# A state space layer: the input product and 6 of the 16 outputs of the gated product in plain float32, these 6 summed chunk by chunk beside the states

## The chip, the cores and the metric

The program runs on one NeuronCore of a Trainium2 chip. The metric is the time of one execution on the device in microseconds (us). The engines that matter here are TensorE (PE, the matrix multiplier, with its weight loads PEld), VectorE (DVE), ScalarE (ACT), GpSimd (POOL), and SyncE (SP), which issues most of the transfers. Each runs its own list of instructions in order, and waits on semaphores for the others. DVE and ACT do elementwise work; PE's sums land in PSUM, eight banks of 2 KB for each of the 128 partitions.

## The reference, cut to what matters

Two models run one after the other. The change is in the second, which has four layers on a sequence of 256 positions and 1024 channels. Each layer is a mixer and a gated feed-forward (`swiglu`), each behind a root-mean-square norm. The mixers are attention (layer 0), the state space layer (1), a pooling layer (2), attention (3).

```python
def s5_layer(h, w_in, a_re, a_im, log_dt, b_re, b_im, c_re, c_im, d, w_glu):
    u = (h @ w_in).astype(F32)
    u_g = u.reshape(B, S, S5_GROUPS, S5_GROUP).astype(jnp.complex64)
...
    bu = jnp.einsum('gpc,bsgc->bsgp', b_bar, u_g)
...
    _, states = lax.associative_scan(combine, (lam_seq, bu), axis=1)
...
    y = jnp.einsum('gcp,bsgp->bsgc', c_mat, states).real.reshape(B, S, D_MODEL)
    y = y + d.astype(F32) * u
    g = jax.nn.gelu(y).astype(h.dtype)
    val, gate = jnp.split(g @ w_glu, 2, axis=-1)
    return val * jax.nn.sigmoid(gate)
```

`w_in` is 1024 x 1024 and `w_glu` 1024 x 2048. There are 64 groups of 16 channels with 64 complex states each. All inputs are float32.

## The kernel before

Activations lie with channels on the partitions: `x[:, k]` is one of eight chunks (KC = 8) of 128 channels by 256 positions (T). A product of a weight tile and an activation is made as three matmuls (`mm3`, L48) in the reduced format fp32r. Each operand is split into a high part and the rest: `piece` (L66) makes `wh` on ACT (a copy in fp32r) and `wl` on DVE (raw minus `wh`) from a raw weight tile that `raw` (L61) loads with a transfer of 1024 KB. The products are wh by high, wh by low and wl by high, and a block of 128 outputs needs 8 x 3 of them. One wh and one wl cover 128 outputs by all 1024 inputs (128x1024). The plain `mm` (L46) on float32 operands is also in the program, in the norms (`ones` as weights).

Around the state space layer, `block2` (L1541 to L1546) calls `s5_table` (it builds tables on POOL and ACT), then `ffn(0)`, the feed-forward of layer 0, then `s5`, then the pooling layer with `ffn(1)`. The Tile scheduler writes each engine's list in the order in which the code issues instructions, with priorities for a few. `s5_table` stands in the code ahead of `ffn(0)`, and so its ACT instruction for `rtab` (tile s5rt, L2125), which copies the decay factor of all 32 state blocks over 128 positions (128x4096), stands on ACT ahead of the first reciprocal root of the norm in `ffn(0)`, `rstd`.

`s5` (L2172) goes through the eight chunks m of 128 channels (eight groups, 512 states). For each chunk:
- **The input product**: `wh`, `wl` of one 128-column piece of `w_in`, and 24 matmuls into a PSUM bank. The activation was left by `prep` (L1594) of `ffn(0)` as two tiles `gh` (ACT) and `gl` (DVE). DVE multiplies by the norm's `rstd` into `u` (L2240).
- **States**: PE makes `bu` from `u` and the transfer `bc` (32 matmul instructions, 32 rows each). DVE multiplies it by a table (tiles `A`, L2197, and `B`, L2198), POOL adds the halves into `Z` (L2199), DVE scans `Z` twice with `rtab` (L2204) and turns it back by the table (again tiles `A` and `B`, L2206 and L2207; each tile name has two buffers). PE makes the outputs of the chunk from `A`, `B`, `u` (72 small matmuls), DVE adds the direct term (`yy`, L2218), ACT takes the gelu, and `split` leaves `yh`, `yl`.
- The three stages of neighbouring chunks overlap by generators (`turn`), which are stepped once a chunk.

After the last input product, `linear` (L1688) makes the 16 blocks of 128 outputs of the gated product (the values m and the gates m of pair m, eight pairs), each from a `wh` and a `wl` piece. A written plan starts the first three of them with the chunks that are ready while the last states run. `emit` (L2249) applies the gate, adds to `x`, and prepares the next norm.

## Time and profile before

| What | us |
|---|---|
| Median of 3 runs | 2117.79 |
| Lowest and highest of the 3 | 2117.03, 2118.68 |
| Time of the profiled execution | 2118.83 |
| Its span in the trace | 2117.0 |
| PE busy, share of the span | 1964.3, 93% |
| DVE busy, share | 1436.8, 68% |
| ACT busy, share | 1044.2, 49% |
| POOL busy, share | 405.9, 19% |

The span is the time from the first to the last instruction in the trace; the time of the execution is 1.83 us longer. Busy shares are means over a program with many different stages, so whether an engine bounds a stage must be read from the windows of that stage. In the span's clock (us from its start), `ffn(0)` begins at about 1050 and `s5` runs from about 1246 to 1384. A matmul's start, and the distance from one start to the next, tell more than its recorded duration, as matmuls are pipelined and overlap.

### The profile page before, as it was taken

The page shows a single profiled execution, that of the slowest core. Times are in us where ns is not written, and L with a number is a line of the kernel's source. Part 1 is how long each engine was busy: PE and PEld are TensorE (multiplying, and loading weights), DVE is VectorE, ACT ScalarE, POOL GpSimd, SP SyncE. Part 2 cuts the span into 40 slices and gives each one's busy share as a digit, 9 for nine tenths or more (in the row PEclk, how much of TensorE's full clock was granted, in tenths as well). Part 3 has the DMA queues.
Part 4 walks back from the last instruction along what each step waited for, and adds up shares of the span by engine and source line. Part 5 has one row for each costly group of instructions (what it writes and reads, how often), then busy time and mean ns, then how long its engine had stood idle before and what let it go on. Part 6 is the DMA issues. An engine that isn't in the chain of part 4 may idle for free.

```text
span 2117.0 us, 36711 instructions
## 1 busy us (share of the span) xinstructions
PE 1964.3 (93%) x14800; PEld 1697.8 (80%) x14803; DVE 1436.8 (68%) x2407; ACT 1044.2 (49%) x1766; POOL 405.9 (19%) x562
## 2 busy tenths in 40 slices
PE   6999897999899879899899996899999999999998
PEld 3666465998585655488899985899999999989998
DVE  4999548998783541298766679866558656767654
ACT  4445635886544531276544442354456444555444
POOL 1001212234100110133289812200010000010000
PEclk9999997999999989999999998999999999999999
DMA  7665136999327959945556552365535554436551
...
DMA packets 275714, 408.87 MB, mean 193 GB/s; under 512 B 10000, under 2 KB 241424, under 8 KB 268240
## 3 DMA queue, kind: packets, MB, share of 16 engines
...
q8 instruction: 119, 1.95, 0.4%
...
HBM read 390.93 MB, written 24.64 MB: 196 GB/s over the span
## 4 chain that ended last, share of the span: by engine, by line
PE 49%; DVE 7%; issue 3%; ACT 2%; POOL 1%; DMA 1%; SPq 0%; DVEq 0%; POOLq 0%; ACTq 0%
PE mm L46 44%; PE gu L46 3%; DVE wl L55 2%; DVE Z L2204 1%; PE py L46 1%; PE px L46 1%; DVE gl L1600 1%; DMA rawx<-in_w_up 1%; POOL x L1580 1%; ACT wh L54 0%; DVE A L2197 0%; PE mm L1833 0%; DMA raw<-in_fox_w_in 0%; DVE A L2206 0%; POOL Z L2199 0%
## 5 line engine op out<-in xcount | busy, mean ns | idle before, releaser
L55 DVE TENSOR_TENSOR wl<-raw,wh 128x1024 fp32r<-128x1024 f32 x476 | 584.3, 1232 | 214.4 <-ACT wh L54 212.2
L54 ACT ACTIVATE wh<-raw 128x1024 fp32r<-128x1024 f32 x476 | 496.4, 1050 | 468.7 <-PE mm L46 263.1
L46 PE MATMUL mm<-gh,wh 128*128 128x256 f32 (+1 forms) x1744 | 497.6, 285 | 2.6 <-ACT wh L54 2.6
L46 PE MATMUL mm<-gh,wl 128*128 128x256 f32 (+1 forms) x1744 | 494.9, 284 | 3.3 <-DVE wl L55 3.3
L46 PE MATMUL mm<-gl,wh 128*128 128x256 f32 (+1 forms) x1744 | 493.9, 283 | 0.3 <-DVE gl L1600 0.3
L46 PEld LDWEIGHTS mm<-gh,wh 128*128 128x128 f32 (+1 forms) x1744 | 330.2, 189 | 6.1 <-ACT wh L54 3.0
L46 PEld LDWEIGHTS mm<-gh,wl 128*128 128x128 f32 (+1 forms) x1744 | 329.8, 189 | 4.9 <-DVE wl L55 4.3
L46 PEld LDWEIGHTS mm<-gl,wh 128*128 128x128 f32 (+1 forms) x1744 | 329.9, 189 | 1.3 <-DVE gl L1600 0.5
L46 PE MATMUL mm<-fh,wh 128*128 128x256 f32 x704 | 199.2, 286 | 3.0 <-DVE x L1640 1.6
L46 PE MATMUL mm<-fl,wh 128*128 128x256 f32 x704 | 199.0, 284 | 0.0
L46 PE MATMUL mm<-fh,wl 128*128 128x256 f32 x704 | 198.5, 284 | 0.0
L1604 POOL TENSOR_TENSOR sq<-sq 128x256 f32<-128x256 f32 x48 | 40.0, 834 | 682.1 <-ACT sq L1602 484.3
L46 PEld LDWEIGHTS mm<-fh,wh 128*128 128x128 f32 x704 | 134.3, 192 | 5.1 <-DVE x L1640 2.4
L46 PEld LDWEIGHTS mm<-fl,wh 128*128 128x128 f32 x704 | 135.0, 192 | 0.3 <-DVE fl L55 0.2
L46 PEld LDWEIGHTS mm<-fh,wl 128*128 128x128 f32 x704 | 134.7, 192 | 0.0
L46 PE MATMUL gu<-wh,gt 128*128 128x256 f32 (+1 forms) x576 | 109.5, 298 | 0.2 <-DVE gt L55 0.2
L1666 DVE TENSOR_TENSOR ft<-mm,rstd 128x512 f32<-128x512 f32 x88 | 60.8, 691 | 52.1 <-PE mm L46 52.1
L54 ACT ACTIVATE fh<-fa 128x256 fp32r<-128x256 f32 x88 | 36.7, 417 | 111.0 <-DVE fa L1669 111.0
L46 PEld LDWEIGHTS gu<-wh,gt 128*128 128x128 f32 (+1 forms) x576 | 87.0, 185 | 3.4 <-DVE gt L55 0.4
L46 PE MATMUL gu<-wl,gt 128*128 128x256 f32 (+1 forms) x320 | 85.6, 311 | 1.3 <-DVE wl L55 1.2
L46 PE MATMUL proj<-xh,wh 128*128 128x512 f32 x208 | 85.1, 410 | 0.0
L46 PE MATMUL proj<-xh,wl 128*128 128x512 f32 x208 | 83.0, 399 | 0.0
...
## 6 DMA issues: line engine op xcount, KB each, us to landing
raw<-in_ffn_w_gate_up SPq DMA_DIRECT2D x88, 1024.0 KB, 5.5
raw<-in_w_ada SPq DMA_DIRECT2D x48, 1024.0 KB, 6.0
raw<-in_ffn_w_down SPq DMA_DIRECT2D x44, 1024.0 KB, 4.9
raw<-in_w_down SPq DMA_DIRECT2D x26, 1024.0 KB, 11.3
raw<-in_fox_w_in SPq DMA_DIRECT2D x24, 1024.0 KB, 5.7
raw<-in_w_in SPq DMA_DIRECT2D x20, 1024.0 KB, 5.4
raw<-in_w_up SPq DMA_DIRECT2D x16, 1024.0 KB, 11.2
raw<-in_w_gate SPq DMA_DIRECT2D x15, 1024.0 KB, 12.3
```

The costliest lines, as they stand in the source:

```text
L46: return self.nc.tensor.matmul(out, a, b, start=start, stop=stop, skip_group_check=True)
L54: self.nc.scalar.activation(hi, src, AF.Copy)
L55: (lo_eng or self.nc.vector).tensor_tensor(lo, src, hi.bitcast(F32), op=ALU.subtract)
L1580: nc.gpsimd.tensor_tensor(x, x, self.rs1, op=ALU.mult)
L1600: nc.vector.scalar_tensor_tensor(self.gl[:, k], x, s, self.gh[:, k].bitcast(F32), op0=ALU.mult, op1=ALU.subtract)
L1604: nc.gpsimd.tensor_tensor(sq, sq, self.sq, op=ALU.add)
L1666: nc.vector.tensor_tensor(t, gu, rs[:, None, :].to_broadcast([P, 2, T]), op=ALU.mult)
L2204: nc.vector.tensor_tensor_scan(z, self.rtab[:, 4 * m:4 * m + 4].rearrange("p a t -> p (a t)"), z, 0.0, ALU.mult, ALU.add)
```

## The change

Five things change; the numbers of lines are those of the changed kernel only in the rows below.

1. **The input product** is 8 plain float32 matmuls a chunk on the weights as loaded, in place of 24 in fp32r. No `wh`, `wl` are made of `w_in`. Its activation is one float32 tile `gf`, which ACT writes in `ffn(0)`; the eight DVE instructions for `gl` go.
2. **Six of the 16 blocks** of the gated product (the pairs 0 to 2, NA = 3) are summed chunk by chunk, as plain float32 matmuls of `yy` on rows of `w_glu` as loaded (`rows`, two transfers of 384 KB for two chunks), into three PSUM banks `acc`. The other ten keep `piece` and `mm3`.
3. **PSUM**: one bank `mm` is shared by the input products and the outputs (there were four), three are `acc`, and `bu` keeps four, which the later blocks take over.
4. **The order** within a chunk is written out in `step(m)`.
5. **`rtab`** is two tiles of four state blocks, written by eight ACT instructions (128x4x127), one for a chunk, in place of one of 128x4096.

```diff
-                with banks(4) as self.pm, tc.tile_pool(name="s5t", bufs=1) as st:
+                    self.ffn(0, self.V["mix"][1], whole=True)
+                with banks(1) as self.pm, tc.tile_pool(name="s5t", bufs=1) as st:
...
         if g is not None:
-            self.gh, self.gl = self.b8("gh"), self.b8("gl")
+            self.gh, self.gl = (self.b8("gf", F32), None) if whole else (self.b8("gh"), self.b8("gl"))
...
             nc.scalar.activation(self.gh[:, k], x, AF.Copy, scale=s)
-            nc.vector.scalar_tensor_tensor(self.gl[:, k], x, s, self.gh[:, k].bitcast(F32), op0=ALU.mult, op1=ALU.subtract)
+            if self.gl is not None:
+                nc.vector.scalar_tensor_tensor(self.gl[:, k], x, s, self.gh[:, k].bitcast(F32), op0=ALU.mult, op1=ALU.subtract)
...
 
-        self.rtab = sp.tile([P, NS, P], F32, name="s5rt")
-        nc.scalar.activation(self.rtab, self.s5r[:, :, None].to_broadcast([P, NS, P]), AF.Copy)
-        nc.gpsimd.memset(self.rtab[:, :, 0:1], 0.0)
+        self.rtab = [sp.tile([P, 4, P], F32, name=f"s5rt{q}") for q in range(2)]
...
+
+        NA = 3
+        accs = lambda: self.pm.tile([P, 2, T], F32, name="acc", tag="acc", bufs=NA)
+        sums, rows, raw = [], {}, {}
...
             bu = bu[:, :, 0:2].rearrange("p a q t -> p q a t")
-            tab = self.tab[:, 4 * m:4 * m + 4].rearrange("p a q t -> p q a t")
             A, B, Z = t("A", four), t("B", four), t("Z", four, 1)
-            nc.vector.tensor_tensor(A, bu, tab, op=ALU.mult)
-            nc.vector.tensor_tensor(B, bu, tab[:, ::-1], op=ALU.mult)
+            nc.vector.tensor_tensor(A, bu, tab(m), op=ALU.mult)
+            done = nc.vector.tensor_tensor(B, bu, tab(m)[:, ::-1], op=ALU.mult)
             nc.gpsimd.tensor_tensor(Z[:, 0], A[:, 0], A[:, 1], op=ALU.add)
             nc.gpsimd.tensor_tensor(Z[:, 1], B[:, 1], B[:, 0], op=ALU.subtract)
-            yield
+            nc.scalar.activation(self.rtab[m % 2][:, :, 1:], self.s5r[:, 4 * m:4 * m + 4, None].to_broadcast([P, 4, P - 1]), AF.Copy)
...
+        def scanned(m, Z):
             for q in range(2):
                 z = Z[:, q].rearrange("p a t -> p (a t)")
-                nc.vector.tensor_tensor_scan(z, self.rtab[:, 4 * m:4 * m + 4].rearrange("p a t -> p (a t)"), z, 0.0, ALU.mult, ALU.add)
+                done = nc.vector.tensor_tensor_scan(z, self.rtab[m % 2].rearrange("p a t -> p (a t)"), z, 0.0, ALU.mult, ALU.add)
...
+        def rest(m):
+            nc.vector.tensor_tensor(yl[:, m], ys[m], yh[:, m].bitcast(F32), op=ALU.subtract)
+
+        def summed(k):
+
+            if not sums:
+                sums.extend(accs() for _ in range(NA))
+            for m in range(NA):
+                for q in range(2):
+                    self.mm(sums[m][:, q], rows[k // 2][:, k % 2, q, m * P:m * P + P], ys[k], k == 0 and q == 0, k == KC - 1)
+
+        after = lambda d: self.tc.issue_after(d.ins)
+        ab = {}
+
+        def step(m):
+
+            k = m - 1
+            done = None
+            if 0 <= k < KC:
+                Z, done = states(k)
+            if k > 1:
+                y = outputs(k - 2, *ab.pop(k - 2))
+                if done:
+                    with after(done):
+                        activated(k - 2, y)
+                else:
+                    activated(k - 2, y)
+            if m < KC:
+                ps = product(m)
+            if 0 <= k < KC:
+                done = scanned(k, Z)
+            if m < KC:
+                done = nc.vector.tensor_tensor(us[m], halves(ps), halves(self.rs), op=ALU.mult)
+            if done:
+                with after(done):
+                    if k > 1:
+                        rest(k - 2)
+                    if 0 <= k < KC:
+                        ab[k] = turned(k, Z)
+            elif k > 1:
+                rest(k - 2)
+            if k > 1:
+                summed(k - 2)
+
...
+        def product(m):
             if m % 2 == 0:
-                raw = self.raw(w[:, :, P * m:P * m + 256], KC, 256)
-            wh, wl = self.piece(raw[:, :, m % 2 * P:m % 2 * P + P], [KC, P])
+                raw[0] = self.raw(w[:, :, P * m:P * m + 256], KC, 256)
+                r = rows[m // 2] = self.wp.tile([P, 2, 2, NA * P], F32, name="raw", tag="raw", bufs=self.wbufs[0])
+                for kk in range(2):
...
             for k in range(KC):
-                self.mm3(ps, wh[:, k], wl[:, k], self.gh[:, k], self.gl[:, k], k == 0, k == KC - 1)
+                self.mm(ps, raw[0][:, k, m % 2 * P:m % 2 * P + P], self.gh[:, k], k == 0, k == KC - 1)
...
-            nc.vector.tensor_tensor(g, ps[0], g, op=ALU.mult)
-            nc.vector.tensor_tensor(self.x[:, m], self.x[:, m], g, op=ALU.add)
-            self.prep(m)
+                    self.norm(lambda: accs()[:, 0])
+            return ps
+
+        for m in range(KC):
+            step(m)
...
+        raws, open_, banks = {}, {}, []
+
+        def part(c, k0, k1):
+            m, q = divmod(c, 2)
+            if c not in open_:
+                if m % 2 == 0:
+                    at = q * D + (NA + m) * P
+                    n = min(256, D - (NA + m) * P)
+                    raws[q] = self.raw(wg[:, :, at:at + n], KC, n)
+                if c == 0:
+                    b = self.pm.tile([P, 4, 2, T], F32, name="bu", tag="bu", bufs=1)
+                    banks.extend(b[:, a] for a in range(4))
+                if c == 8:
+                    banks.append(accs())
+                open_[c] = self.piece(raws[q][:, :, m % 2 * P:m % 2 * P + P], [KC, P])
+            wh, wl = open_[c]
+            for k in range(k0, k1):
+                self.mm3(banks[m][:, q], wh[:, k], wl[:, k], yh[:, k], yl[:, k], k == 0 and q == 0, k == KC - 1)
+
         self.prep_begin(gnext)
-        self.linear([wg[:, :, q * D:q * D + D] for q in range(2)], yh, yl, emit, rest(), (None, (0, 0, 5), None, (1, 0, 5), (2, 0, 5), (0, 5, 6), (1, 5, 6), None, (2, 5, 6), (0, 6, 7), (1, 6, 7), (2, 6, 7)))
+        step(KC)
+        for c in range(3):
+            part(c, 0, 5)
+        step(KC + 1)
+        for c in range(3):
+            part(c, 5, 7)
+        step(KC + 2)
+        for m in range(NA):
+            emit(m, sums[m])
+        for c in range(2 * (KC - NA)):
+            part(c, 7 if c < 3 else 0, KC)
+            if c % 2:
+                emit(NA + c // 2, banks[c // 2])
         self.prep_end()
```

ACT at the start of `ffn(0)`, with the semaphores that each row waits for (DMASW are transfers that POOL issued, here the stores of `s5_table`'s inputs). Before:

```order
L54 ACTIVATE wh_10537<-raw_10454 128x1024 [waits PE_49,Activation_49]
L1599 ACTIVATE gh_9846<-x_58,cols_6818 128x256 [waits DVE_49]
L1602 ACTIVATE sq_10151<-x_58 128x256 [waits Pool_49]
L2125 ACTIVATE s5rt_10168<-s5r_8430 128x4096 [waits DMASW5_49,DMASW4_49,DMASW6_49,DMASW3_49,DMASW2_49]
L1584 ACT_TABLE_LOAD
L1584 ACTIVATE rstd_10480<-mm_10477,eps_94 128x256 [waits PE_49]
L54 ACTIVATE wh_10565<-raw_10456 128x1024 [waits PE_49,Activation_49]
L54 ACTIVATE wh_10637<-raw_10630 128x1024 [waits DMAHW5_49,PE_49,Activation_49]
```

and now:

```order
L54 ACTIVATE wh_10538<-raw_10455 128x1024 [waits PE_49,Activation_49]
L1600 ACTIVATE gh_9846<-x_58,cols_6818 128x256 [waits DVE_49]
L1604 ACTIVATE sq_10151<-x_58 128x256 [waits Pool_49]
L54 ACTIVATE wh_10533<-raw_10459 128x1024 [waits DMASW5_49,DMASW6_49,DMASW4_49,DMAHW4_49,DMASW3_49,DMASW2_49]
L1584 ACT_TABLE_LOAD
L1584 ACTIVATE rstd_10481<-mm_10478,eps_94 128x256 [waits PE_49]
L54 ACTIVATE wh_10566<-raw_10457 128x1024 [waits PE_49,Activation_49]
L54 ACTIVATE wh_10627<-raw_10459 128x1024
```

The instruction for s5rt is gone from ahead of `rstd`; in its place stands `wh_10533`, the high part of down-projection weights, which stood eleven rows further up before. It waits for the same five transfers of POOL's.

PE in one chunk of `s5`. Before, from the outputs of a chunk (tile mm_13073) over the `bu` of a later one to the next input product (mm_13156):

```order
L46 MATMUL mm_13073<-A_13010,bc_12762 32x127 x4
L46 MATMUL mm_13073<-A_13010,bc_12762 32x128 x4
L46 MATMUL mm_13073<-A_13010,bc_12762 32x127 x4
L46 MATMUL mm_13073<-B_13011,bc_12762 32x128 x4
L46 MATMUL mm_13073<-B_13011,bc_12762 32x127 x4
L46 MATMUL mm_13073<-B_13011,bc_12762 32x128 x4
L46 MATMUL mm_13073<-B_13011,bc_12762 32x127 x4
L46 MATMUL bu_13121<-u_12935,bc_12936 128x128 x16
L46 MATMUL mm_13156<-gh_12522,wh_13147 128x256
L46 MATMUL mm_13156<-gl_12523,wh_13147 128x256
L46 MATMUL mm_13156<-gh_12522,wl_13148 128x256
```

and now, from the outputs (mm_12989) to the next `bu` (`acc` are the sums of the six blocks, `raw_12744` the rows of `w_glu`, `gf` the activation):

```order
L46 MATMUL mm_12989<-A_12852,bc_12748 32x127 x4
L46 MATMUL mm_12989<-A_12852,bc_12748 32x128 x4
L46 MATMUL mm_12989<-A_12852,bc_12748 32x127 x4
L46 MATMUL mm_12989<-B_12853,bc_12748 32x128 x4
L46 MATMUL mm_12989<-B_12853,bc_12748 32x127 x4
L46 MATMUL mm_12989<-B_12853,bc_12748 32x128 x4
L46 MATMUL mm_12989<-B_12853,bc_12748 32x127 x4
L46 MATMUL mm_13035<-gf_12523,raw_12931 128x256 x8
L46 MATMUL acc_12856<-yy_13026,raw_12744 128x256 x2
L46 MATMUL acc_12857<-yy_13026,raw_12744 128x256 x2
L46 MATMUL acc_12858<-yy_13026,raw_12744 128x256 x2
L46 MATMUL bu_13058<-u_13030,bc_13031 128x128 x16
```

The input product now stands between the outputs and the `bu`, its 24 matmuls are 8, and six sums follow it.

DVE in one chunk. Before:

```order
L2197 TENSOR_TENSOR A_13031<-bu_13014,s5tab_10167 128x1024
L2198 TENSOR_TENSOR B_13032<-bu_13014,s5tab_10167 128x1024
L2204 SCALAR_TENSOR_TENSOR Z_13033<-s5rt_10168,Z_13033 128x512
L2240 TENSOR_TENSOR u_13042<-mm_13047,rstd_12680 128x256
L2204 SCALAR_TENSOR_TENSOR Z_13033<-s5rt_10168,Z_13033 128x512
L55 TENSOR_TENSOR wl_13438<-raw_13435,wh_13437 128x1024
L2206 TENSOR_TENSOR A_13117<-Z_13033,s5tab_10167 128x1024
L2218 SCALAR_TENSOR_TENSOR yy_13110<-u_12761,cols_6818,mm_13073 128x2x128
L2207 TENSOR_TENSOR B_13118<-Z_13033,s5tab_10167 128x1024
L55 TENSOR_TENSOR yl_12652<-yy_13110,yh_12651 128x256
L2197 TENSOR_TENSOR A_13138<-bu_13121,s5tab_10167 128x1024
```

and now, from the chunk k = 3 to the chunk k = 4:

```order
L2206 TENSOR_TENSOR A_12981<-bu_12964,s5tab_10167 128x1024
L2207 TENSOR_TENSOR B_12982<-bu_12964,s5tab_10167 128x1024
L2239 SCALAR_TENSOR_TENSOR yy_13026<-u_12747,cols_6818,mm_12989 128x2x128
L2216 SCALAR_TENSOR_TENSOR Z_12983<-s5rt0_10168,Z_12983 128x512 x2
L2275 TENSOR_TENSOR u_13030<-mm_13035,rstd_12663 128x256
L2244 TENSOR_TENSOR yl_12644<-yy_13026,yh_12643 128x256
L2221 TENSOR_TENSOR A_13048<-Z_12983,s5tab_10167 128x1024
L2222 TENSOR_TENSOR B_13049<-Z_12983,s5tab_10167 128x1024
L55 TENSOR_TENSOR wl_13336<-raw_13332,wh_13335 128x1024
L2206 TENSOR_TENSOR A_13075<-bu_13058,s5tab_10167 128x1024
L2207 TENSOR_TENSOR B_13076<-bu_13058,s5tab_10167 128x1024
```

The chunk's `wl` of an input weight is gone. `yy` moved ahead of the scans and `u` behind them. In this chunk, a `wl` of the first piece of `w_glu` that is still split stands ahead of the next chunk's `A`; its raw tile takes the buffer that the input product's weights had.

## Rows read from the trace of the kernel before

**Rows 1.** Windows of the start of ffn(0): us and instructions per engine, granted clock, DMA
```profile
1060.00:1070.00 10.00, 8.70 (x44) 8.40 (x44) 7.93 (x10) 4.20 (x7) 9.29 (x14) 0.54 0.37 110
1070.00:1240.00 170.00, 169.99 (x1427) 169.74 (x1427) 109.40 (x119) 75.04 (x99) 125.25 (x190) 1.00 0.59 196
```

**Rows 2.** Timeline of ACT at the start of ffn(0): start, duration, idle before and releaser
```profile
1051.22 3.63 ACT L2125 ACTIVATE s5rt<-s5r 128x4096 f32<-128x4096 f32 x1 [3.70 <-DMA bcd<-s5m]
...
1056.53 3.89 ACT L54 ACTIVATE wh<-raw 128x1024 fp32r<-128x1024 f32 x4
```

**Rows 3.** Timeline of DVE at the same place
```profile
1056.66 1.75 DVE L1585 RECIPROCAL rstd<-rstd 128x256 f32<-128x256 f32 x1 [8.46 <-ACT rstd L1584]
1058.33 1.16 DVE L55 TENSOR_TENSOR wl<-raw,wh 128x1024 fp32r<-128x1024 f32 x1
```

**Rows 4.** Timeline of PE at the same place
```profile
1057.63 0.38 PE L46 MATMUL mm<-gh,wh 128*128 128x256 f32 x1 [2.25 <-ACT wh L54]
...
1059.55 0.58 PE L46 MATMUL mm<-gh,wl 128*128 128x256 f32 x1 [1.42 <-DVE wl L55]
...
1060.15 0.42 PE L46 MATMUL mm<-gl,wh 128*128 128x256 f32 x1
...
1064.20 0.41 PE L46 MATMUL mm<-gh,wl 128*128 128x256 f32 x1
```

**Rows 5.** Timeline of DVE, from the first state chunk to the last
```profile
1252.27 1.23 DVE L55 TENSOR_TENSOR wl<-raw,wh 128x1024 fp32r<-128x1024 f32 x1 [0.22 <-ACT wh L54]
...
1255.05 1.23 DVE L55 TENSOR_TENSOR wl<-raw,wh 128x1024 fp32r<-128x1024 f32 x1 [0.56 <-ACT wh L54]
1256.19 1.22 DVE L2197 TENSOR_TENSOR A<-bu,s5tab 128x1024 f32<-128x1024 f32 x1
...
1275.60 1.21 DVE L2197 TENSOR_TENSOR A<-bu,s5tab 128x1024 f32<-128x1024 f32 x1
...
1277.86 0.40 DVE L2240 TENSOR_TENSOR u<-mm,rstd 128x256 f32<-128x256 f32 x1
1278.26 3.39 DVE L2204 TENSOR_TENSOR_SCAN Z<-s5rt,Z 128x512 f32<-128x512 f32 x2
1281.57 1.19 DVE L55 TENSOR_TENSOR wl<-raw,wh 128x1024 fp32r<-128x1024 f32 x1
1282.68 0.47 DVE L2218 SCALAR_TENSOR_TENSOR yy<-u,cols,mm 128x256 f32<-128x256 f32 x1
...
1285.68 1.21 DVE L2197 TENSOR_TENSOR A<-bu,s5tab 128x1024 f32<-128x1024 f32 x1
...
1326.00 1.22 DVE L2197 TENSOR_TENSOR A<-bu,s5tab 128x1024 f32<-128x1024 f32 x1
```

**Rows 6.** Timeline of PE inside the state space layer
```profile
1278.04 2.09 PE L46 MATMUL bu<-u,bc 32*128 32x128 f32 x32 [2.70 <-issue]
...
1294.36 1.08 PE L46 MATMUL mm<-A,bc 128*32 128x128 f32 x32 [1.66 <-DVE A L2206]
1295.89 1.08 PE L46 MATMUL mm<-B,bc 128*32 128x128 f32 x32 [0.45 <-DVE B L2207]
1298.54 1.17 PE L46 MATMUL bu<-u,bc 32*128 32x128 f32 x32 [1.57 <-issue]
1299.64 0.39 PE L46 MATMUL mm<-gh,wh 128*128 128x256 f32 x1
...
1315.18 1.93 PE L46 MATMUL mm<-A,bc 128*32 128x128 f32 x32 [4.71 <-DVE A L2206]
```

**Rows 7.** Timeline of PE in an earlier norm: plain float32 matmuls
```profile
902.14 1.24 PE L46 MATMUL ssq<-s,ones 128*128 128x256 f32 x5
```

**Rows 8.** Groups of POOL instructions in the layer, by form
```profile
L2199 POOL TENSOR_TENSOR Z<-A 128x512 f32<-128x512 f32 x8 | 10.2, 1274 | 61.3 <-DVE A L2197 61.3
```

**Rows 9.** DMA issues in the layer: count, KB, median us to landing
```profile
raw<-in_s_w_glu SPq DMA_DIRECT2D x6, 1024.0 KB, 5.3
```

**Rows 10.** Timeline of PE at the end of the layer
```profile
1384.01 0.28 PE L46 MATMUL mm<-yh,wl 128*128 128x256 f32 x1
```

More of the change, by code (lines that the diff above doesn't have):

```diff
@@ L1611, in prep_end, with norm @@
         self.rs = None
-    def norm(self):
+    def norm(self, bank=None):
         if self.rs is None:
-            ps = self.bank([P, T])
+            ps = bank() if bank else self.bank([P, T])
             for q in range(2):
@@ L1620, in norm, with ffn @@
         return self.rs
-    def ffn(self, l, gnext, lag=3, each=None, aside=None):
+    def ffn(self, l, gnext, lag=3, each=None, aside=None, whole=False):
         nc, i = self.nc, self.i
@@ L1630, in ffn @@
             left = self.ffn_body(fp, w, wd, n, acc, gh, gl, lag, aside)
-            self.prep_begin(gnext)
+            self.prep_begin(gnext, whole)
             first = 2 if lag > 2 else 5
@@ L2216, in states, with activated @@
                     self.mm(y[strip(a), 0, 1:], bc[:, even, strip(a)], v[:, q, a, 0:P - 1], False, n == 3)
[L2217 to L2218 removed]
+            return y
+        def activated(m, y):
+            yy = ys[m] = t("yy", [P, T])
+            nc.vector.scalar_tensor_tensor(halves(yy), us[m], self.V["d"][:, m:m + 1], y, op0=ALU.mult, op1=ALU.add)
             nc.scalar.activation(yy, yy, AF.Gelu_apprx_tanh)
[L2220 removed]
@@ L2222, in turn @@
-        def turn(*new):
-            live[:] = [g for g in [*live, *new] if next(g, self) is not self]
-        raw = None
-        for m in range(KC):
+            nc.scalar.activation(yh[:, m], yy, AF.Copy)
+        def rest(m):
[6 more added lines that the diff above has]
+                    self.mm(sums[m][:, q], rows[k // 2][:, k % 2, q, m * P:m * P + P], ys[k], k == 0 and q == 0, k == KC - 1)
```

48 lines of the change are left out of this document (24 added, 24 removed).

## The prediction, made before the changed kernel ran

> **What bounds the kernel now.** I read the windows over the program first, then the timelines of the engines in the two places that the change touches.
>
> The first place is the start of `ffn(0)`. Once it runs, PE is busy for 169.99 of 170 us at the full clock, 1427 matmuls, so 0.119 us for each [rows 1]. Whatever is saved ahead of that stretch reaches the end whole. Ahead of it time is lost. ACT waits for a transfer, fills the table s5rt for 3.63 us, and only then comes to `rstd` [rows 2]. DVE's reciprocal waits 8.46 us for that and takes 1.75, and then the next `wl` 1.16 [rows 3]. PE runs dry twice, for 2.25 and 1.42 us, and what comes next is slow: from 1060.15 to 1064.20 the 19 steps take 0.213 us each, against 0.119 [rows 4]. [...]
>
> The second place is `s5`. One chunk takes 10.08 us on DVE, from one `A` to the next (1275.60 to 1285.68), without a hole: `A` and `B` 2.26 together, `u` 0.40, two scans 3.31, `wl` 1.11, `yy` 0.47, `A` and `B` again, `yl` [rows 5]. PE waits for DVE there (1.66, 0.45, 1.57 us in one chunk, and once 4.71) [rows 6]. From the first `A` (1256.19) to the last (1326.00) it is 69.8 us, and 58.1 more to the layer's last matmul at 1384.01 plus 0.12 [rows 5, 10].
>
> **The change, part by part.**
>
> *1. The start of `ffn(0)`.* s5rt (3.63) leaves; in its slot, behind the same transfers, stands one `wh`, a quarter of 3.89 = 0.97 [rows 2]. So `rstd` is 2.66 us earlier, and so are the reciprocal and the `wl` behind it (the `wl` at about 1055.7 to 1056.8). PE's first gap (2.25) goes, as the `wh` that it waited for is there at 1055.0; the second, for `wl`, stays at some 1.4. Whether the low clock comes after one gap of 1.4 the rows leave open: gaps of 1.66 and 1.57 in `s5` were followed by a `bu` of 1.17 us and a matmul step at full speed, gaps of 2.70 and 4.71 by a `bu` of 2.09 and a slow group of 1.93 in place of 1.08 [rows 6]. If it stays away, the 4.76 go as well, but for a wait for the next stage's operand that may be left and that I put at up to 1 us: -2.25 - 3.76 = -6.0, and -7.0 without that wait. If it comes, the gain is the 2.66 alone. Each of the eight new ACT instructions for s5rt costs about 3.63 / 8 = 0.45 (an estimate), in a stage where ACT is idle more than half the time (75.04 busy of 170 us [rows 1]). I take **-6.5**, with -2.6 and -8.4 as its ends.
>
> *2. Into the layer.* `wl` at 1252.27 and 1255.05 stand ahead of the first `u` and the first `A` [rows 5] and go: 2 x 1.2 = 2.4 us, so the first `A` is at 1253.8 of the old clock. The first two chunks have no outputs yet. DVE does `A`, then waits for POOL, whose two halves of `Z` take 1.27 each [rows 8] and end some 2.66 after `A`'s start, then scans 3.31, `u` 0.40, `A` and `B` 2.26: 8.63, twice, so the third `A` is at 1271.1, 4.5 us ahead of 1275.60.
>
> *3. The chunks from then on: DVE is no longer alone on the path.* DVE's own work would be 2.26 + 0.47 + 3.31 + 0.40 + 0.40 + 2.26 = 9.1 [rows 5]. But PE now does, in order and through one shared bank, outputs, input product, six sums, `bu`. The price of a plain float32 matmul is in [rows 7]: five records of 128x256, the last 0.38 long by the tile's median, start over 1.24 - 0.38 = 0.86 us, so 0.215 apart, and each matmul leaves two such records, so 0.43, against 3 x 0.119 = 0.356 for the three in fp32r that it replaces. After `A` starts: `yy` empties the bank at 2.26 + 0.47 = 2.73; product 8 x 0.43 = 3.45, to 6.3; sums 6 x 0.43 = 2.6, to 8.9; `bu` 1.10 (1298.54 to 1299.64 [rows 6]), to 10.0; then the outputs by `u` and `A` (0.2 and 1.08 [rows 6]), to 11.2 or 11.3. Only then is the buffer free that the next `A` writes, since the name has two. So a chunk takes **11.3**, longer than the 10.1 of before; PE is busy for about 2.2 + 3.45 + 2.6 + 1.1 = 9.3 of it and idle for 2.
>
> In one chunk more is late: the `wl` of `w_glu` stands on DVE ahead of the fifth-to-sixth `A`. Its raw tile is loaded into the buffer that the product frees at 6.3; 5.3 to land [rows 9], `wh` 1.0, `wl` 1.2: 13.8, so about 14.1 in that chunk, with nearly 5 us without work for PE. The gap of 4.71 in [rows 6] was followed by the low clock; the same here makes the next product and sums dearer. All of a chunk's 28 float32 records at the low level would cost 4.8 more (worked out under rival A); I take two thirds, 3.2, as the low level need not last for all of them. In the last chunk two `wl` add 0.4.
>
> Sum: 1271.1 + 11.3 x 3 + 14.1 + 11.7 = 1330.8 for the last `A`, 1334.0 with the low clock once: +4.8 or **+8.0** against 1326.00.
>
> *4. From the last `A` to the last matmul.* `yy` at 2.7 and gelu 0.4; six sums to 5.8; the three opened blocks over five chunks, less the eight matmuls done while PE waited, 37 x 0.119 = 4.4; outputs 2.1; `yy` and gelu 0.9; sums 2.6; six more steps of three blocks 2.1; outputs 2.1; `yy`, gelu 0.9; sums 2.6: 23.5. Then the last step of three blocks 1.1, about 1.4 for a `wh` and a `wl` that find their buffers only now, and seven blocks x 24 x 0.119 = 20.0: 46.0. Before it was 58.1 with 16 blocks by `wh` and `wl`: **-12.1**.
>
> *5. Into `ffn(1)`.* The DVE work on the pooling layer's constants, spread over the layer's tail before, now stands behind it: 0 to 1.5, I take **+0.5**.
>
> Sum: -6.5 + 8.0 - 12.1 + 0.5 = -10.1. The profiled execution's 2118.83 is 1.04 above the shown median, its span 2117.0; against the median that is 2117.79 - 10.1 = **2107.7**.
>
> [...]
>
> **The rivals.**
>
> *A, slower: PE falls to the low clock in every chunk from the third on.* The place is the hole of about 2 us that each chunk now has on PE. For it: PE's time is now on the chunk's path, and gaps little wider did it. Against it: 1.57 and 1.66 did not, and the hole may come in two pieces. Each chunk's 14 float32 matmuls are 28 records; the fp32r step went from 0.119 to 0.213 [rows 1, 4], a factor of 1.8, so 28 x 0.215 x 0.8 = 4.8 more. Over five chunks 24, less the 3.2 counted: -10.1 + 20.8, so **2128.5**. It decides from 2.0 us a chunk on average (10.1 / 5); two or three chunks in the low clock end near 2114 to 2118.
>
> *B, the start of `ffn(0)` gives only the 2.66.* For it: the gap of 1.42 that stays was followed by the low clock, if behind another. Time: 2107.7 + 3.9 = **2111.6**.
>
> *C, DVE alone sets the chunk*: `A` is not held up by the outputs, or the sums run elsewhere. Then five chunks take 9.1, 45.5 in place of 62.9: **2090**. Against it is the order of PE and the two buffers.
>
> *D, the raw tile comes in time* and no low clock comes: 14.1 becomes 11.3 and 3.2 goes: -6.0, so **2101.7**.
>
> **How the numbers follow.** The forecast, with the clock falling once or so: 0.45 (2104 to 2111). B 0.18, D 0.14, C 0.06, A in two or three chunks 0.09, A in full 0.08. Under 0.2%, 4.2 us, is about what a measurement of this kernel can't tell from no change, so "faster" is below 2113.6. It holds the forecast, B, C and D less a little: 0.81; "same" 0.10; "slower" 0.09. The range leaves out C below, and full A and some of the lesser A above: 2098 to 2116.
>
> **What would show it.** Right: no s5rt ahead of `rstd`, its start near 1053.5; PE's granted clock in the ten us behind it near 1; starts of `A` 8.6 apart twice, then 11.3, once 14; pairs of records of `mm<-gf,raw` 0.215 apart; 46 from the last `A` to the last matmul of the layer. Wrong: low granted clock in the chunks (A); `A` to `A` of 9 (C); 16 or more us in the chunk with the `wl`, if the load queues behind others; a `wh` on ACT that holds up gelu and so the sums.

## The result, and the profile after

The changed kernel takes 2128.52 us (median of 6 runs, 2127.21 to 2132.74), the kernel before in the same set 2119.10 (6 runs, 2117.03 to 2120.89): a ratio of 1.0052, with an interval of 1.0042 to 1.0062. It is slower by 9.4 us, where 10.1 less were forecast; the time lies outside the range.

The profiled execution took 2132.74 us, its span is 2130.9. It is compared with before by distances inside each trace, since what comes ahead of the change already differs by 3.1 us between the two (at the first mark below the runs of this document lie between 1043.1 and 1050.8, whichever kernel it is). Three rows of before that were not shown ahead serve as marks, timeline of DVE: the end of the layer-0 mixer, the reciprocal of the state space layer's norm, and the reciprocal of the next norm.

```profile
1047.73 0.47 DVE L1600 SCALAR_TENSOR_TENSOR gl<-x,cols,gh 128x256 fp32r<-128x256 f32 x1
...
1250.30 1.75 DVE L1585 RECIPROCAL rstd<-rstd 128x256 f32<-128x256 f32 x1 [1.45 <-ACT rstd L1584]
...
1391.49 1.75 DVE L1585 RECIPROCAL rstd<-rstd 128x256 f32<-128x256 f32 x1
```

The same three of the changed kernel:

```profile
1050.84 0.48 DVE L1602 SCALAR_TENSOR_TENSOR gl<-x,cols,gh 128x256 fp32r<-128x256 f32 x1
...
1246.74 1.75 DVE L1585 RECIPROCAL rstd<-rstd 128x256 f32<-128x256 f32 x1 [2.67 <-ACT rstd L1584]
...
1404.48 1.73 DVE L1585 RECIPROCAL rstd<-rstd 128x256 f32<-128x256 f32 x1
```

From the first to the second, `ffn(0)`, it was 202.57 us and is 195.90: 6.7 gained. From the second to the third, the layer, it was 141.19 and is 157.74: **16.6 lost**. What follows differs by little: 213.9 to 215.2 for `ffn(1)` up to its reciprocal, under half a us after.

**The start of `ffn(0)`**, the timeline of ACT and the windows (us, then busy time and instructions of PE, PEld, DVE, ACT, POOL, then the granted clock, DMA share, GB/s), answers to [rows 1, 2]:

```profile
1052.30 1.06 ACT L54 ACTIVATE wh<-raw 128x1024 fp32r<-128x1024 f32 x1 [1.93 <-DMA bcd<-s5m]
...
1054.67 0.47 ACT L1584 ACTIVATE rstd<-mm,eps 128x256 f32<-128x256 f32 x1
```

```profile
1055.00:1060.00 5.00, 5.00 (x45) 5.00 (x44) 4.82 (x5) 4.98 (x6) 3.04 (x4) 1.00 0.36 115
1060.00:1070.00 10.00, 7.78 (x53) 7.38 (x52) 8.45 (x9) 5.79 (x10) 9.37 (x13) 0.83 0.74 246
```

`rstd` comes 1.3 us of table load after one `wh` of 1.06, where s5rt took 3.63. PE has no hole between 1055 and 1060 (5.00 of 5 us busy), and the ten us behind have a granted clock of 0.83 in place of 0.54. It is not 1.00 there, as two holes have come later, each of 1.11 us, for the next stage's `fh` and `fl` (timeline of PE):

```profile
1062.19 0.39 PE L46 MATMUL mm<-fh,wh 128*128 128x256 f32 x1 [1.11 <-ACT fh L54]
...
1063.69 0.58 PE L46 MATMUL mm<-fl,wh 128*128 128x256 f32 x1 [1.11 <-DVE fl L55]
```

Behind the second one twelve steps are about 0.213 us apart, which costs some 1.1 us against 0.119.

**The chunks**, timeline of DVE, the rows of each first `A` and of the `wl` of `w_glu`, answers to [rows 5]:

```profile
1250.40 1.23 DVE L2206 TENSOR_TENSOR A<-bu,s5tab 128x1024 f32<-128x1024 f32 x1 [1.30 <-PE bu L46]
...
1258.90 1.21 DVE L2206 TENSOR_TENSOR A<-bu,s5tab 128x1024 f32<-128x1024 f32 x1
...
1267.78 1.23 DVE L2206 TENSOR_TENSOR A<-bu,s5tab 128x1024 f32<-128x1024 f32 x1 [0.25 <-PE mm L46]
...
1281.04 1.22 DVE L2206 TENSOR_TENSOR A<-bu,s5tab 128x1024 f32<-128x1024 f32 x1 [1.92 <-PE mm L46]
...
1294.25 1.22 DVE L2206 TENSOR_TENSOR A<-bu,s5tab 128x1024 f32<-128x1024 f32 x1 [1.92 <-PE mm L46]
...
1307.40 1.23 DVE L55 TENSOR_TENSOR wl<-raw,wh 128x1024 fp32r<-128x1024 f32 x1 [3.50 <-ACT wh L54]
1308.54 1.22 DVE L2206 TENSOR_TENSOR A<-bu,s5tab 128x1024 f32<-128x1024 f32 x1
...
1322.21 1.22 DVE L2206 TENSOR_TENSOR A<-bu,s5tab 128x1024 f32<-128x1024 f32 x1 [1.92 <-PE mm L46]
...
1335.47 1.23 DVE L2206 TENSOR_TENSOR A<-bu,s5tab 128x1024 f32<-128x1024 f32 x1 [1.92 <-PE mm L46]
```

The steps are 8.50, 8.88, then 13.26, 13.21, 14.29, 13.67, 13.26. The first two are the forecast's. The others were to be 11.3, the one with the late `wl` 14.1 and the last 11.7. DVE now waits for PE's outputs for 1.92 us ahead of `A` in four of them, and for `wh` for 3.50 in the one with the `wl`. From the third `A` to the last it is 67.7 us, where before it was 50.4.

PE in the chunks of 13.21 and 14.29 us, timeline, the input products, answers to [rows 6, 7]:

```profile
1283.88 5.38 PE L46 MATMUL mm<-gf,raw 128*128 128x256 f32 x16 [2.04 <-issue]
...
1297.14 3.69 PE L46 MATMUL mm<-gf,raw 128*128 128x256 f32 x16 [2.09 <-DVE yy L2239]
```

The 16 records of the input product take 5.38 us in the first and 3.69 in the second. Inside the product of the chunk before (13.26 us), timeline of PE, the records that run between 1271.9 and 1274.5:

```profile
1271.40 3.57 PE L46 MATMUL mm<-gf,raw 128*128 128x256 f32 x8
```

This product begins at 1270.67, after a hole of 2.09, at the full clock (a granted 0.98 up to 1271.40), and three records later falls to the low one (0.52 from there to 1274.90): these eight take 3.57 with the last one 0.58 long, so they start 0.427 apart, twice the 0.215 of [rows 7]. Eight records at 0.21 more are 1.7 us. Three of the five products show this. A fourth, at 1311.38 behind the late `wl`, has a hole of 4.76 ahead, is slow from its start and takes 2.15 us longer than the fast one, from its start to the sums. The fifth (1297.14) has the same hole of 2.09 ahead as the three and no slow record; what makes the difference no run here shows.

**The tail**, timeline of PE, to the layer's last matmul:

```profile
1359.37 0.47 PE L46 MATMUL bu<-yh,wh 128*128 128x256 f32 x1
...
1365.43 0.58 PE L46 MATMUL bu<-yh,wh 128*128 128x256 f32 x1 [5.00 <-DVE g L2292]
...
1373.71 0.55 PE L46 MATMUL bu<-yh,wh 128*128 128x256 f32 x1 [2.62 <-DVE g L2292]
...
1382.27 0.39 PE L46 MATMUL acc<-yh,wh 128*128 128x256 f32 x1 [1.08 <-ACT wh L54]
...
1383.53 0.39 PE L46 MATMUL acc<-yh,wl 128*128 128x256 f32 x1 [0.76 <-DVE wl L55]
...
1396.18 0.28 PE L46 MATMUL acc<-yh,wl 128*128 128x256 f32 x1
```

and the timeline of DVE at the first two holes:

```profile
1364.96 0.41 DVE L2292 TENSOR_TENSOR g<-bu,g 128x256 f32<-128x256 f32 x1
...
1373.24 0.42 DVE L2292 TENSOR_TENSOR g<-bu,g 128x256 f32<-128x256 f32 x1
```

From the last `A` (1335.47) to the layer's last matmul (1396.18 and 0.12 to the next start) it is 60.8 us, where the forecast had 46.0 and before had 58.1. The sums of the last chunk end at 1359.37, 23.9 after that `A` (forecast 23.5). Then PE does six matmuls and stands still for 5.00 us, until DVE has read the finished pair 3 (`g`, 1364.96 and 0.41 long), and for 2.62 us until it has read pair 4 (1373.24). The records behind each of these two holes are at the low clock, 0.213 us apart, and so are some behind two shorter holes, where PE waits for `wh` and `wl`. The windows show how long (columns as above):

```profile
1360.00:1370.00 10.00, 5.00 (x25) 4.80 (x24) 7.79 (x13) 6.42 (x13) 2.46 (x3) 0.68 0.51 158
1370.00:1380.00 10.00, 7.38 (x48) 7.17 (x47) 3.11 (x5) 3.21 (x5) 0.73 (x1) 0.81 0.31 105
1380.00:1390.00 10.00, 8.17 (x54) 7.76 (x53) 3.36 (x6) 3.21 (x5) 0.73 (x1) 0.83 0.64 212
```

PE does 25, 48 and 54 matmuls in ten us each; 0.119 apart they would be 84. The two waits for `g` are 7.6 us, the two shorter holes 1.8, and some 50 slow steps cost 4.7. The names of the rows say why it waits: the pairs 3 to 6 are slices of one tile `bu`. The matmuls for pair 4 write another slice than the one that DVE reads, and stand behind that reading all the same; the runs `tail` and `gates` below test whether that is the cause.

### The profile page after: what moved, and what is told of

The parts are those of the page before. It is cut to its first block, busy times and chain, and to the rows that moved or that the text cites. A ratio compares the mean times of both kernels' runs of the same rounds, so it can differ in the third digit from the quotient of the medians.

```text
span 2130.9 us, 36470 instructions
## 1 busy us (share of the span) xinstructions
PE 1977.7 (93%) x14691; PEld 1701.6 (80%) x14691; DVE 1416.3 (66%) x2385; ACT 1031.9 (48%) x1759; POOL 406.4 (19%) x563
## 4 chain that ended last, share of the span: by engine, by line
PE 44%; DVE 4%; ACT 1%; issue 1%; POOL 0%; DMA 0%; DVEq 0%; ACTq 0%; POOLq 0%
PE mm L46 40%; PE bu L46 2%; DVE wl L55 1%; PE acc L46 1%; DVE gl L1602 0%; DVE A L2206 0%; DVE Z L2216 0%; ACT wh L54 0%; DVE rstd L1585 0%; POOL sq L1606 0%; DVE B L2207 0%; PE mm L1835 0%; DVE x L1642 0%; DMA bcd<-s5m 0%; DVE x L1725 0%
## 5 line engine op out<-in xcount | busy, mean ns | idle before, releaser
L55 DVE TENSOR_TENSOR wl<-raw,wh 128x1024 fp32r<-128x1024 f32 (+1 forms) x462 | 567.7, 1234 | 222.6 <-ACT wh L54 221.1
L54 ACT ACTIVATE wh<-raw 128x1024 fp32r<-128x1024 f32 (+1 forms) x462 | 481.5, 1050 | 478.5 <-PE mm L46 250.3
L46 PE MATMUL mm<-gh,wh 128*128 128x256 f32 (+1 forms) x1680 | 477.5, 284 | 0.5 <-ACT wh L54 0.5
L46 PE MATMUL mm<-gh,wl 128*128 128x256 f32 (+1 forms) x1680 | 475.3, 283 | 2.2 <-DVE wl L55 2.2
L46 PE MATMUL mm<-gl,wh 128*128 128x256 f32 (+1 forms) x1680 | 474.8, 283 | 0.2 <-DVE gl L1602 0.2
L46 PEld LDWEIGHTS mm<-gh,wl 128*128 128x128 f32 (+1 forms) x1680 | 316.8, 189 | 3.6 <-DVE wl L55 3.2
L46 PEld LDWEIGHTS mm<-gh,wh 128*128 128x128 f32 (+1 forms) x1680 | 317.0, 189 | 3.2 <-issue 1.8
L46 PEld LDWEIGHTS mm<-gl,wh 128*128 128x128 f32 (+1 forms) x1680 | 316.8, 189 | 1.3 <-DVE gl L1602 0.4
L1668 DVE TENSOR_TENSOR ft<-mm,rstd 128x512 f32<-128x512 f32 x88 | 60.8, 691 | 52.1 <-PE mm L46 52.1
## 6 DMA issues: line engine op xcount, KB each, us to landing
raw<-in_w_up SPq DMA_DIRECT2D x16, 1024.0 KB, 11.1
```

The lines of the kernel that those rows point to most:

```text
L46: return self.nc.tensor.matmul(out, a, b, start=start, stop=stop, skip_group_check=True)
L54: self.nc.scalar.activation(hi, src, AF.Copy)
L55: (lo_eng or self.nc.vector).tensor_tensor(lo, src, hi.bitcast(F32), op=ALU.subtract)
L1668: nc.vector.tensor_tensor(t, gu, rs[:, None, :].to_broadcast([P, 2, T]), op=ALU.mult)
```

## The experiments

Theory 1 was that two things cost the time, apart from each other: the wait on the one tile in the tail, and the hole in each chunk with the low clock behind it; and that the eight-piece table alone gains what is gained. The rivals were that float32 passes are simply too dear, or that only the places in the order matter.

### Banks of their own in the tail (tail)

```diff
                 if c == 0:
                     b = self.pm.tile([P, 4, 2, T], F32, name="bu", tag="bu", bufs=1)
-                    banks.extend(b[:, a] for a in range(4))
-                if c == 8:
+                    banks.extend(b[:, a] for a in range(2))
+                if c > 3 and c % 2 == 0:
                     banks.append(accs())
...
-            if c % 2:
+            if c == 3:
+                emit(NA, banks[0])
+            if c > 2 and c % 2:
                 emit(NA + c // 2, banks[c // 2])
```

> The changed kernel, with the pairs 5 to 7 of the gated product in the banks of the sums (tile acc, one tile each) in place of slices of the one tile bu, and with the gates of pairs 3 and 4 after the fourth block; nothing is left out. Theory 1 (in the layer's tail PE waits at each pair until DVE has read the pair before out of the same tile, and falls to the low clock after each of these waits): the holes of 5.0 and 2.6 us and the low clock behind them go, from the last A to the layer's last matmul it is about 48 us in place of 61, and the time is 10 to 14 us below the changed kernel's, so about 2116. Theory 2 (the float32 passes and the split weights of ten blocks are simply too much for PE and ACT there, the wait on the tile is only where the lateness shows): the holes move to waits for wh or wl, and under 3 us come back.

Measured: 2112.93 us (10 runs), 15.6 below the changed kernel and so somewhat more than expected; against the kernel before a ratio of 0.9978, interval 0.9968 to 0.9988. The last `A` (timeline of DVE):

```profile
1330.91 1.23 DVE L2206 TENSOR_TENSOR A<-bu,s5tab 128x1024 f32<-128x1024 f32 x1 [1.92 <-PE mm L46]
```

the last matmul of the layer (timeline of PE):

```profile
1377.30 0.28 PE L46 MATMUL acc<-yh,wl 128*128 128x256 f32 x1
```

and a window behind the last sums:

```profile
1365.00:1378.00 13.00, 13.00 (x111) 13.00 (x111) 11.47 (x15) 8.51 (x16) 3.22 (x4) 1.00 0.92 314
```

It is 46.5 us from the last `A`, with PE at the full clock, and from 1365 on without a hole. The forecast's 46.0 was right for a kernel without that wait; the wait and the clock behind it cost 14.3. The edit has two parts, and the next run parts them.

### Only the place of the gates (gates)

```diff
-            if c % 2:
+            if c == 3:
+                emit(NA, banks[0])
+            if c > 2 and c % 2:
                 emit(NA + c // 2, banks[c // 2])
```

> The changed kernel with only one of the two edits to the tail: the gates of pair 3 come after the fourth block, so that they stand with those of pair 4; all of the pairs 3 to 6 stay slices of the one tile bu. Theory 1 (PE waits for DVE's reading of another slice of the same tile): one of the waits goes, the others stay at the next pairs, each with a hole of 2.5 us or more and a stretch of low clock behind it, and the time stays 5 us or more above the 2112.9 of the kernel in which the pairs have tiles of their own. Theory 2 (it was the place of the gates, or of wh and wl, in the order): the whole gain comes with this edit alone, within 2 us of 2112.9.

Measured: 2122.59 us (10 runs), 5.9 below the changed kernel and 9.7 above `tail`. Timeline of PE:

```profile
1363.10 0.58 PE L46 MATMUL bu<-yh,wh 128*128 128x256 f32 x1 [4.54 <-DVE g L2292]
```

Of the two holes that wait for DVE's `g` one is gone, and one of 4.54 us stays. `tail` differs from this kernel in the tiles alone, so the 9.7 us between them are the shared tile's: theory 1 holds. The expectation that each of the other waits would keep a hole over 2.5 us was not met, there is one.

### Filling the hole in the chunks with matmuls on zeros (fill)

```diff
+            if k > 2 and m < KC:
+                for _ in range(5):
+                    self.mm(sums[0][:, 0], zero, ys[k - 3], False, False)
             if m < KC:
                 ps = product(m)
```

> The changed kernel with five more float32 matmuls in each chunk from the fourth on, with weights that are zero, added into a sum between the outputs and the input product, where PE waits some 2.1 us for yy; the result is not changed by them, nothing is left out. Theory 1 (the low clock that begins in the input product comes from this hole, and costs 1.7 us in each of the chunks): the 0.43 us steps of records in the input product go back to 0.216, the chunk of 13.2 becomes 11.4 to 11.6 where the filling just fits, and the time falls by 3 to 6 us against the changed kernel. Theory 2 (the low clock there comes from the whole chunk's little work or from the float32 products themselves, not from the hole): the slow records stay, and the chunk is as long or longer, up to 2 us each, since the filling delays the product.

Measured: 2123.10 us (6 runs), 5.4 below the changed kernel. Timeline of PE, one chunk:

```profile
1276.77 2.43 PE L46 MATMUL acc<-yy,zero 128*128 128x256 f32 x10
1279.04 3.62 PE L46 MATMUL mm<-gf,raw 128*128 128x256 f32 x16
```

The product takes 3.62 us in place of 5.38, and the chunk to which these rows belong is 11.60 us long, by DVE's first `A`. The first of the five products in this run has no zeros ahead of it and serves for comparison: behind its hole of 2.09 us it still takes 5.38. The four with zeros ahead take 3.62 to 3.69. So the low clock came from the hole, and a chunk without it is close to the 11.3 that the forecast worked out. The zeros did keep the clock up.

### The eight-piece table alone, on the kernel before (rtab)

```diff
-        self.rtab = sp.tile([P, NS, P], F32, name="s5rt")
-        nc.scalar.activation(self.rtab, self.s5r[:, :, None].to_broadcast([P, NS, P]), AF.Copy)
-        nc.gpsimd.memset(self.rtab[:, :, 0:1], 0.0)
+        self.rtab = [sp.tile([P, 4, P], F32, name=f"s5rt{q}") for q in range(2)]
+        for r in self.rtab:
+            nc.gpsimd.memset(r[:, :, 0:1], 0.0)
...
+            nc.scalar.activation(self.rtab[m % 2][:, :, 1:], self.s5r[:, 4 * m:4 * m + 4, None].to_broadcast([P, 4, P - 1]), AF.Copy)
```

> The kernel before with one part of the change alone: the table s5rt written in eight pieces in the chunks, in place of one of 3.63 us ahead of the norm of ffn(0). Theory 1 (this alone is what the start of ffn(0) gains): rstd starts 2.6 us earlier against the last norm chunk before it, no long low clock follows, and the time is 5 to 7 us below the kernel before, so 2112 to 2114. Theory 2 (the gain comes from elsewhere, such as the split of the activation that is no longer made, or the new instructions cost ACT as much in the chunks as they give): under 2 us.

Measured: 2106.68 us (6 runs), 11.7 below the kernel before; ratio 0.9948, interval 0.9936 to 0.9960. That is more than either theory said. Windows at the start of `ffn(0)`:

```profile
1060.00:1070.00 10.00, 8.89 (x73) 8.69 (x74) 8.17 (x9) 4.66 (x7) 9.45 (x12) 1.00 0.75 258
```

No low clock follows there (1.00 for 0.54), and from the first mark to the second it is 195.71 us, 6.9 less than before, as in the changed kernel. But the layer, from the second mark to the third, is 135.71 us long for 141.19: 5.5 came in the tail, where the part does nothing by itself (from the second mark to the last `A` the two kernels differ by 0.15 us).

### Where the other 5.5 came from (consts, consts2)

In the kernel before, 34 DVE instructions for the pooling layer's constants run from 1335.74 to 1359.94, while the state space layer's last chunk and first blocks are made, and the last chunk's `yy` starts at 1340.77 behind 15 of them. PE waits 4.57 us for the `yh` that follows from it (timelines of DVE and PE, kernel before):

```profile
1335.74 0.46 DVE L1862 TENSOR_SCALAR cnt<-cnt 128x16 f32<-128x16 f32 x1 [0.46 <-POOL cnt L1861]
...
1340.77 0.47 DVE L2218 SCALAR_TENSOR_TENSOR yy<-u,cols,mm 128x256 f32<-128x256 f32 x1
...
1342.19 1.00 PE L46 MATMUL mm<-yh,wh 128*128 128x256 f32 x3 [4.57 <-ACT yh L54]
```

With the smaller table they all come after the layer's last addition to `x`. Both runs hold these instructions back in the kernel before with its table in one piece:

```diff
+        with self.tc.issue_after(self.s5done.ins):
+            it = ct.tile([P, 16], I32, name="it")
...
-            nc.gpsimd.iota(di, pattern=[[1, T]], base=-P * j, channel_multiplier=-1)
+            with self.tc.issue_after(self.s5done.ins):
+                nc.gpsimd.iota(di, pattern=[[1, T]], base=-P * j, channel_multiplier=-1)
...
-            nc.vector.tensor_tensor(self.x[:, m], self.x[:, m], g, op=ALU.add)
+            self.s5done = nc.vector.tensor_tensor(self.x[:, m], self.x[:, m], g, op=ALU.add)
```

> The kernel before with the pooling layer's constants on POOL and DVE held back until the state space layer's last addition to x; the table s5rt stays in one piece, nothing is left out. Theory 1 (of the 11.7 us that the eight-piece table gave, 6.9 came at the start of ffn(0) and some 5 in the layer's tail, because the constants no longer stand on DVE ahead of the last yy, yl and wl): the wait of 4.6 us for yh in the tail goes, 4 to 6 us below the kernel before. Theory 2 (all of it came from the start of ffn(0), the tail's 5 are the clock's chance): within 1.5 us of the kernel before.

Measured: 2117.49 us (11 runs), ratio 0.9995, interval 0.9986 to 1.0004: no difference. But the edit had not done what it was for. Timeline of DVE:

```profile
1338.39 0.52 DVE L1874 TENSOR_SCALAR dge<-d 128x256 f32<-128x256 f32 x1 [3.13 <-POOL d L1873]
1338.95 1.43 DVE L1878 SCALAR_TENSOR_TENSOR band<-d,dge 128x256 f32<-128x256 f32 x4
1340.30 0.48 DVE L2220 SCALAR_TENSOR_TENSOR yy<-u,cols,mm 128x256 f32<-128x256 f32 x1
```

Five of the constants stayed ahead of `yy`, and the first waited 3.13 us for POOL. `consts2` puts the rest of `bands` under the same `issue_after`, here against `consts`:

```diff
             with self.tc.issue_after(self.s5done.ins):
                 nc.gpsimd.iota(di, pattern=[[1, T]], base=-P * j, channel_multiplier=-1)
-            nc.gpsimd.tensor_copy(d, di)
-            v.tensor_scalar(ge, d, 0.0, None, op0=ALU.is_ge)
+                nc.gpsimd.tensor_copy(d, di)
+                v.tensor_scalar(ge, d, 0.0, None, op0=ALU.is_ge)
...
+                with self.tc.issue_after(self.s5done.ins):
...
```

> The kernel before with all of the pooling layer's constants on DVE and POOL held back until the state space layer's last addition to x; in the earlier try of this, the first five of them on DVE still stood ahead of the last yy and waited 3.1 us for POOL. The table s5rt stays in one piece, nothing is left out. Theory 1 (of the 11.7 us of the eight-piece table, some 5 came from the tail, where the constants no longer stand ahead of the last yy, yl and wl): yy of the last chunk starts within 1 us of its outputs' end, the wait of 4.6 us for yh goes, and the time is 4 to 6 us below the kernel before. Theory 2 (the start of ffn(0) alone made it): within 1.5 us of the kernel before.

Measured: 2110.23 us (6 runs), ratio 0.9962, interval 0.9947 to 0.9977: 8.0 below the kernel before, by the interval 5 to 11, where theory 1 said 4 to 6. Timeline of DVE:

```profile
1336.63 0.48 DVE L2221 SCALAR_TENSOR_TENSOR yy<-u,cols,mm 128x256 f32<-128x256 f32 x1 [0.87 <-PE mm L46]
```

The last `yy` now waits for PE's outputs alone, 0.87 us, PE's wait for `yh` is gone, and the layer is 134.83 us long between the marks, 6.4 less than before. (In this execution `ffn(0)`, which the edit does not touch, is 1.3 us shorter as well.) That is at least as much as the table gained there: the 5.5 are the constants' place, and that they moved is a side effect of the smaller table. By which rule the scheduler moved them was not tried.

### The input product alone (product)

`rtab` and the float32 input product, with the old order, four shared banks and all 16 blocks by `wh` and `wl`:

```diff
-            wh, wl = self.piece(raw[:, :, m % 2 * P:m % 2 * P + P], [KC, P])
...
-                self.mm3(ps, wh[:, k], wl[:, k], self.gh[:, k], self.gl[:, k], k == 0, k == KC - 1)
+                self.mm(ps, raw[:, k, m % 2 * P:m % 2 * P + P], self.gh[:, k], k == 0, k == KC - 1)
```

> The kernel before with two parts of the change: the eight-piece table, and the input product in float32 on weights as loaded, with the old order, four shared banks and all 16 blocks by wh and wl. Theory 1 (the float32 product by itself helps, since DVE bounds the chunk and loses a wl; what costs is the order with one bank, the sums and the one tile in the tail): a chunk of 10.1 to 10.4 becomes 9.0 to 9.4, the time is 6 to 10 us below the 2106.7 of the table alone. Theory 2 (float32 passes are what costs, by their 0.43 for 0.356 and by a low clock): no gain or a loss against 2106.7.

Measured: 2106.86 us (4 runs), the same as the 2106.68 of the table alone; against the kernel before both have a ratio of 0.9948. Timeline of DVE, one chunk:

```profile
1286.58 0.47 DVE L2220 SCALAR_TENSOR_TENSOR yy<-u,cols,mm 128x256 f32<-128x256 f32 x1
1287.98 0.43 DVE L55 TENSOR_TENSOR yl<-yy,yh 128x256 fp32r<-128x256 f32 x1 [0.93 <-ACT yh L54]
1288.32 1.22 DVE L2198 TENSOR_TENSOR A<-bu,s5tab 128x1024 f32<-128x1024 f32 x1
...
1290.98 3.39 DVE L2206 TENSOR_TENSOR_SCAN Z<-s5rt,Z 128x512 f32<-128x512 f32 x2 [0.32 <-POOL Z L2200]
...
1298.62 1.22 DVE L2198 TENSOR_TENSOR A<-bu,s5tab 128x1024 f32<-128x1024 f32 x1
```

The chunk is still 10.3 us. The `wl` of 1.1 is gone, but in this order `yl` stands right behind `yy` and DVE waits 0.93 us for ACT's gelu and copy, and 0.32 for POOL's `Z`. Theory 1 was wrong: DVE's work became less and its chunk did not. The time is theory 2's, its reason isn't: the chunk ahead of this one, in which PE's product took 5.51 us at the low clock, is as long (10.29 us) as this one (10.30), where it took 3.72; PE's passes are hidden there. The equal times are also a sum of two small differences: `ffn(0)` is 1.0 us shorter than in `rtab`, and the layer 2.2 longer, as two `wl` of `w_glu` now stand on DVE in the first chunk, which is 12.40 us long from `A` to `A`.

### The sums one chunk later, and both edits (later, later_tail)

```diff
             if k > 1:
                 y = outputs(k - 2, *ab.pop(k - 2))
...
+            if k > 2:
+                summed(k - 3)
             if m < KC:
                 ps = product(m)
...
-            if k > 1:
-                summed(k - 2)
```

> The changed kernel with the sums of a chunk issued one chunk later, ahead of the input product and so in PE's hole while it waits for yy; nothing is left out. Theory 1 (the chunk's path is outputs, yy, product, sums, bu, outputs, and the hole brings the low clock): the path is shorter by what of the sums moves into the hole, 1.7 to 2.1 us, and the low clock's 1.7 go too; a chunk of 13.2 becomes 10 to 10.6, and the time is 10 to 15 us below the changed kernel's. Theory 2 (DVE or the transfers set the chunk): the chunk stays above 12.5.

Measured: 2111.89 us (7 runs), 16.6 below the changed kernel; 10 to 15 were expected.

> The changed kernel with both edits of before: the sums of a chunk one chunk later, in PE's hole, and the pairs 5 to 7 in the banks of the sums. Theory 1 (the loss is two separate ones, in the chunks and in the tail): the two gains of 16.6 and 15.6 us add but for 2 or 3 us, so 2098 to 2100, below the kernel before by 19 and below the kernel before with the eight-piece table (2106.7) too. Theory 2 (both edits free the same wait, as the clock recovers once in either): the gains don't add, 2108 or more.

Measured: 2095.56 us (4 runs); against the kernel before a ratio of 0.9898, interval 0.9883 to 0.9914. The two gains add in full (16.6 and 15.6; 33.0 together), and the kernel beats the one before by 23.6 (by the interval 18 to 25) and the table alone by 11.1. Timeline of PE, one chunk:

```profile
1289.24 1.05 PE L46 MATMUL mm<-A,bc 128*32 128x128 f32 x32
...
1291.10 1.99 PE L46 MATMUL acc<-yy,raw 128*128 128x256 f32 x8
1293.21 3.69 PE L46 MATMUL mm<-gf,raw 128*128 128x256 f32 x16
1296.74 1.03 PE L46 MATMUL acc<-yy,raw 128*128 128x256 f32 x4
```

and two first `A` on DVE:

```profile
1280.53 1.23 DVE L2206 TENSOR_TENSOR A<-bu,s5tab 128x1024 f32<-128x1024 f32 x1 [0.20 <-PE mm L46]
...
1290.37 1.23 DVE L2206 TENSOR_TENSOR A<-bu,s5tab 128x1024 f32<-128x1024 f32 x1 [0.20 <-PE mm L46]
```

Two thirds of the sums (the scheduler leaves one pair behind the product) stand in PE's hole between the outputs and the product, and a chunk is 9.84 us. What it gains over the table alone does not lie in the chunks, though: from the third `A` to the last it is 53.0 us here and 50.4 in `rtab`. It lies on the way into the layer (from the norm's reciprocal to the third `A` 21.1 us for 25.4) and in the tail (from the last `A` to the last matmul 44.7 for 51.7), which six of the 16 blocks have left.

## Why the prediction was wrong, point by point

- **The start of `ffn(0)` (step 1): the size right, one reading and one hole wrong.** Forecast -6.5, measured -6.7, and -6.9 with the table alone. The gap of 2.25 did not bring the low clock of [rows 4], as the prediction read them: the two matmuls behind it have a granted clock of 1.00, and 0.50 begins behind the next gap, of 1.42. The second hole did not stay at 1.4 either; two of 1.11 came later. The 4.76 in the sum of this step is shown by no run as such: it is an estimate, the ten us of the window of 0.54 in [rows 1] less its 44 matmuls at 0.119, and with the gaps of 2.25 and 1.42 it makes the end of -8.4. By the same estimate the ten us from 1060 on lose 3.7 in the changed kernel (53 matmuls, 0.83) and 1.3 in `rtab` (73 matmuls, 1.00). That the low clock would then stay away was a choice, and not a safe one: in the changed kernel twelve slow steps followed these holes, in `rtab` holes of 1.12 and 1.11 left the clock at 1.00.
- **Into the layer (step 2): right.** 8.63 forecast, 8.50 and 8.88 measured, and the first `A` 3.66 us after the reciprocal for 5.89. The third `A` comes 4.3 us earlier behind the reciprocal, for 4.5.
- **The chunks (step 3): the path right, the clock mis-sized.** I took the low clock once, behind the hole of nearly 5 us, at 3.2 us; there it cost 2.15, and it came in three more of the five chunks at 1.7. The chunk without it was worked out as 11.3 and is 11.6 in `fill`. That is rival A, but with 1.7 to 2.15 a chunk where I had priced 4.8: only 8 to 10 of 28 records were slow. (Each slow one cost 0.21, so twice its time, where I had taken a factor of 1.8.) From the third `A` to the last that is 67.7 for 62.9, so 4.8 us: 4.0 from the clock, the rest from the longer chunk. The chunk with the late `wl` was 14.1 and is 14.29, with some luck: in `tail` and `gates`, where its product falls to the low clock too, it is 16.0.
- **The tail (step 4): the step that failed.** The sum of work, 46.0, is right (46.5 in `tail`), and measured were 60.8. What it left out is a wait that no row of before could show: the pairs 3 to 6 share one tile, so the pairs 4 and 5 wait for the gates of the pair before, 5.00 and 2.62 us, and the low clock follows. It cost 14.3 us. The diff showed it, in `banks.extend(b[:, a] for a in range(4))`; before, each block had a tile of its own. I asked what each matmul costs and when each weight is ready, and not what the bank that it writes waits for.
- **The base of the tail, too, was read too simply.** The 58.1 of before held 6.4 us of delay by the pooling layer's constants: in `consts2` it is 51.7. They went by the table's side effect, and the sum counted all of the 12.1 as the work's merit.
- **Into `ffn(1)` (step 5): low.** +0.5 forecast; measured +0.8 from the last matmul to the reciprocal, and +1.3 from there to the next reciprocal.
- **The rivals.** The time is that of A in full, 2128.5, but by chance, since the causes are others: A's clock in the chunks cost 7.2 us, of which the forecast had counted 3.2, where A in full has 24, and the tail's wait, which was no rival of mine, cost 14.3. B, C and D did not come.
